# Block 2's attention emitted as a pipeline over heads, with TensorE held to the order of emission

## The chip, the cores and the metric

One core of one Trainium2 chip runs the whole program in one launch. The metric is device time in microseconds (us). The kernel is written in Python for a tile framework: the program traces instructions for five engines (TensorE for matrix multiplies and transposes, VectorE for elementwise work and reductions, ScalarE for activation functions and copies, GpSimd, SyncE for DMA issues), a scheduler puts the instructions of each engine into one fixed order, and on the chip every engine works through its own order and waits on semaphores where an operand or a buffer is not ready.

## The reference, cut to what matters

The program computes two transformer blocks in float32 on 512 tokens of width 1024. The change is in the second block, in two of its three attention branches:

```python
h = rms_norm(x, g_norm);  proj = h @ w_in          # q_a k_a v_a ... z_a c_q c_kv ... gate_logits
# branch a: 8 heads of 64, causal and restricted to the top 256 keys of an index score
q_a = partial_rope(rms_norm(q_a, g_qn_a)); k_a = partial_rope(rms_norm(k_a, g_kn_a))
o_a = dsa_attention(q_a, k_a, v_a, q_i, k_i, w_i)  # softmax(q k^T + mask) v, in blocks of 128 queries
# branch b: 8 heads of 96 (64 + 32 rotary), values of 64, causal
q_b = rms_norm(rms_norm(c_q) @ w_uq, g_qn_b); k_b = rms_norm([k_nope, k_rope], g_kn_b)   # then rotary
o_b = causal_attention(q_b, k_b, v_b)
# branch m: cross attention on a memory of 256 tokens
ys = [o_a * silu(z_a), o_b * silu(z_b), o_m * silu(z_m)]
merged = sum over n of sigmoid(gate_logits_n) * (ys_n @ w_branch_n)
x = x + merged @ w_out
```

## The kernel before

**Dense work.** A float32 product of the dense layers is made of three matmuls in the fast float32 form: both operands are split into a high and a low part, and high-high, high-low and low-high are added up in PSUM (`dense`, `dense_tok`). A weight slice is loaded into `wraw`, ScalarE writes its high part `whi`, VectorE the low part `wlo` (`unit`, with high priority). One step of a dense stream is 24 matmuls as a rule: eight slices of 128 rows by three.

**Attention.** Scores of one head for a block b of 128 queries go against the 128(b+1) keys up to that block, b = 0 to 3. `attend` makes one unit, a pair of heads e = 0, 1 for one block. For each head: the scores into a PSUM bank; VectorE adds the mask, writes the result `at_sm` and takes the row maximum `at_mx` in one instruction (L1567); ScalarE takes the exponential with the sum `at_su`; VectorE takes the reciprocal (L1552) and multiplies (`normalise`); TensorE turns the 128x128 pieces into a second bank (`tr`, L191); and that is copied to `at_pt`, by VectorE for e = 0 and by ScalarE for e = 1. After the second head the unit's value products follow (`mm`, L188, tile `y`): 2(b+1) float32 products of 64 columns, each of which stands as two instructions in the trace. When the four blocks of a pair j are done, `branch_in` multiplies the sums by the gate and splits the product into high and low part. PSUM has eight banks; block 2 uses tags mm (2 banks) and q (2) in turn for dense sums (`pm`), y (1) for the attention's output, and p, p, s (3 in all) in turn for scores and transposes (`pt`).

**Streams.** Generators yield after each step, and `weave` draws from several of them: it takes next the one whose count of yields, divided by its number of units, is smallest (`units`, `woven`); a stream that yields None waits, and another is drawn from. The last weave of block 2 (L2048) has three streams: `last_cols` (dense; DU = 53), `attns` (AU = 92, traced with a priority offset AP of 2000 instructions) and `topk` (98; 48 pairs of VectorE's max and match-replace on the index scores, which make the mask of branch a). `attns` does, in order, branch b's heads 0 to 3 (`latent_attn(0)`), then norms, rotary and transposes of the queries and keys of heads 4 to 7 (`latent_prep(1)`), their attention, the norms, rotary and transposes of branch a's queries and keys (`sparse_prep`), and branch a's attention (`sparse_attn`: 4 pairs by 4 blocks). `last_cols` makes the projections that those need (`latent_cols(1)`, `run`), the gates `za`, and the gated sums of branches m and b (`branch`) and the gates of branch a (`gates_a`). `need` lets a stream wait until a name stands in the table T.

**What sets TensorE's order.** In this weave `self.pinned` is empty: dense matmuls are chained to one another in the order in which they are traced (`mmd`), and transposes, scores and value products are placed among them by the scheduler, which goes by priority and by its own forecast of when each is ready. Earlier parts of the kernel set `self.pinned` to "p" (`pin`, L198): then every TensorE instruction is tied behind the one traced before it.

**Places.** `head_norm` L1519, `attend` L1555, `branch_in` L1588, `topk` L1757, `latent_prep` L1872, `latent_attn` L1887, `sparse_prep` L1902, `sparse_attn` L1937, `last_cols` L2027, `attns` L2038, the weave L2048.

Of the kernel before, what the change touches and what calls it, by code (L numbers as in the profile page):

```python
# [18 lines left out]
NB = S // 128  # L19
# [6 lines left out]
PRI, AP = 2000, 2000  # L26
# [8 lines left out]
DU, AU = 53, 92  # L35
# [64 lines left out]
class Build:  # L100
# [1418 lines left out]
    def head_norm(self, pool, x, heads, dim, g, nb=4):  # L1519

        ss = self.tile(pool, [128, 32], "hn_ss", 2)[:, 0:nb * heads]
        n = heads * dim
        for b in range(nb):
            sq = self.tile(self.late or pool, [128, 512], "t2", T2)
            self.act(sq[:, :n], x[:, b], AF.Square)
            self.nc.vector.tensor_reduce(ss[:, heads * b:heads * b + heads],
                                         sq[:, :n].rearrange("p (h d) -> p h d", h=heads), AX.X, OP.add)
        self.ts(ss, ss, 1.0 / dim, 1e-6)
        r = self.rsqrt(pool, ss, nb * heads)
        for b in range(nb):  # L1530
            xv = x[:, b].rearrange("p (h d) -> p h d", h=heads)
            self.mul(xv, xv, r[:, heads * b:heads * b + heads, None].to_broadcast([128, heads, dim]))
            self.mul(xv, xv, g[:, None, :].to_broadcast([128, heads, dim]))

# [20 lines left out]
    def attend(self, pool, b, score, v, mask, O):  # L1555
# [3 lines left out]
        n = 128 * (b + 1)  # L1559
        mx = self.tile(pool, [128, 2], "at_mx", 2)  # L1560
        sums = self.tile(pool, [128, 2], "at_su", 2)
        pts = []
        for e in range(2):
# [3 lines left out]
            nc.vector.tensor_tensor_reduce(sm[:, 0:n], p[:, 0:n], mask[:, 0:n], -1.0, 3e38,  # L1567
# [3 lines left out]
            self.normalise(sm[:, 0:n], sums[:, e:e + 1])  # L1571
            p = self.pt()
# [7 lines left out]
            pts.append(PT)  # L1580
            if e:
                for s in range(b + 1):
                    for c in range(2):
                        self.mm(O[64 * c:64 * c + 64, 128 * b:128 * b + 128], v(c, s),
                                pts[c][:, 128 * s:128 * s + 128], s == 0, s == b)
            yield e
# [9 lines left out]
    def block2(self, main, late, xT, kept, out):  # L1596
# [3 lines left out]
        with tc.tile_pool(name="by", bufs=1, reuse_waits=RW) as py, tc.tile_pool(name="b2", bufs=1, reuse_waits=RW) as p2, xd as dram:  # L1600
# [271 lines left out]
            def latent_prep(hf):  # L1872
                for n, name, tag in (("qb", "lq", "s2"), ("kb", "lk", "s3")):
                    yield from need((name, hf))
                    src = T[name, hf]
                    self.head_norm(p2, src, 4, 96, gains[n])
                    self.rope(p2, src.rearrange("p b (h d) -> p b h d", h=4)[:, :, :, 64:96], 4, 8, 16)
                    dst = T[n] = slot(tag, [96, 4, S])
                    yield 0
# [7 lines left out]
            def latent_attn(hf):  # L1887
# [4 lines left out]
                for j in range(2):  # L1892
                    O = self.pt("y")
                    for b in range(NB):
                        n = 128 * (b + 1)
                        yield from self.attend(
                            p2, b, lambda e, p: self.mm(p[:, 0:n], qT[:, 2 * j + e, 128 * b:128 * b + 128], kT[:, 2 * j + e, 0:n]),
                            lambda e, s: vt[:, s, 2 * j + e], cm[:, 384 - 128 * b:512], O)
                    self.branch_in(O, *(t[:, 2 * hf + j] for t in (T["zb"], *T["b"])))


            def sparse_prep(e, n):  # L1902
                yield from need("t" + n)
                t = T["t" + n]
                self.head_norm(p2, t, 8, 64, gains[n])
                self.rope(p2, t.rearrange("p b (h d) -> p b h d", h=8)[:, :, :, 0:16], 8, 0, 8)
                yield 0
                if e == 0:
# [28 lines left out]
            def sparse_attn():  # L1937
# [9 lines left out]
                for j in range(4):  # L1947
                    O = self.pt("y")
                    for b in range(NB):
                        mask = cm[:, 384:512] if b == 0 else madd[:, moff[b]:moff[b] + 128 * (b + 1)]  # L1950
                        yield from self.attend(p2, b, lambda e, p: score(j, b, e, p),
                                               lambda e, s: va[:, s, 128 * j + 64 * e:128 * j + 64 * e + 64], mask, O)

                    self.branch_in(O, *(t[:, j] for t in (T["za"], *T["a"])))
                    T["ya", j] = True
# [58 lines left out]

            tk = topk()
# [97 lines left out]
```

## Time and profile before

| | |
|---|---|
| time, median of 3 runs | 1573.21 us (1572.8 to 1574.99) |
| the profiled execution's own time | 1564.84 us |
| its span, first to last instruction | 1563.1 us |
| TensorE's mean granted clock | 0.995 |
| TensorE matmul busy | 1523.2 us (97%), 8487 instructions |
| TensorE weight load busy | 1234.9 us (79%) |
| VectorE busy | 1087.7 us (70%), 2536 instructions |
| ScalarE busy | 749.3 us (48%) |
| chain that ended last | PE 82%, DVE 10%, ACT 3%, DMA 2%, issue 2% |

How to read it: PE is TensorE's matmul, PEld its weight load, DVE is VectorE, ACT ScalarE, POOL GpSimd. A matmul's end is modelled and matmuls are pipelined, so the record of one overlaps the next: a PE that is busy for a whole window may still be late. What a matmul costs is the distance from its start to the next one's start. The last weave of block 2 runs from about 1136 us to 1500 us of the span; its attention is between 1141 and 1470 us.

### The profile page before, as it was taken

Reading aid. Unit: us, or ns where it says so; the run is one execution under the profiler, and the core shown is the slowest. Engines: PE = TensorE matmul, PEld = TensorE weight load, DVE = VectorE, ACT = ScalarE, POOL = GpSimd, SP = SyncE. Lnnn points to the kernel's source line nnn. Section 1 sums busy time; section 2 is a strip of 40 time slices with the busy share of each in tenths; the row PEclk is TensorE's granted clock in tenths of the full one; section 3 lists DMA queues with packets and bytes.
Section 4 is the critical chain, followed back from the end, with each engine's and each line's share of the span. In section 5 each row is a group of like instructions: output and inputs, shape, how many; then the busy total and the mean of one; then the engine's idle time right before and its main releaser. Section 6 shows DMA issues by size and latency. Waiting matters only on the chain.

```text
span 1563.1 us, 23743 instructions
## 1 busy us (share of the span) xinstructions
PE 1523.2 (97%) x8487; PEld 1234.9 (79%) x8487; DVE 1087.7 (70%) x2536; ACT 749.3 (48%) x1469; POOL 101.0 (6%) x241
## 2 busy tenths in 40 slices
PE   6999999999999999999999999999999999999999
PEld 5777787788788888888888888888877778777787
DVE  7776697889757565534544578879998758765563
ACT  5645555456455444433432444456554445543431
POOL 7000402121000000000000001000000000000000
PEclk9999999999999999999999999999999999999999
DMA  7533122135534133333333334242322213224232
GB/s 249 142 72 81 48 64 53 39 92 147 170 93 131 41 94 92 97 96 100 95 97 99 92 105 106 65 117 77 90 62 66 70 52 85 77 65 128 62 96 100
DMA packets 209591, 144.85 MB, mean 93 GB/s; under 512 B 13492, under 2 KB 190787, under 8 KB 208960
## 3 DMA queue, kind: packets, MB, share of 16 engines
q1 hardware_dynamic: 208000, 141.66, 32.1%
q0 software_dynamic: 1280, 1.52, 0.4%
q8 instruction: 67, 1.10, 0.3%
q14 instruction: 52, 0.43, 0.1%
q10 hardware_dynamic: 192, 0.14, 0.0%
HBM read 134.90 MB, written 8.39 MB: 92 GB/s over the span
## 4 chain that ended last, share of the span: by engine, by line
PE 82%; DVE 10%; ACT 3%; DMA 2%; issue 2%; SPq 0%; DVEq 0%; ACTq 0%
PE mm L180 38%; PE q L180 27%; PE p L188 4%; PE p L191 3%; PE y L188 3%; DVE wlo L158 2%; PE s L188 2%; PE s L180 2%; PE q L188 2%; PE s L191 1%; PE q L191 1%; DVE St L158 1%; DVE lqk L158 1%; ACT whi L155 1%; DMA kvraw<-k_kept 1%
## 5 line engine op out<-in xcount | busy, mean ns | idle before, releaser
L155 ACT ACTIVATE whi<-wraw 128x512 fp32r<-128x512 f32 (+2 forms) x472 | 292.2, 621 | 499.6 <-PE mm L180 206.2
L158 DVE TENSOR_TENSOR wlo<-wraw,whi 128x512 fp32r<-128x512 f32 (+2 forms) x472 | 320.5, 680 | 187.9 <-ACT whi L155 180.3
L180 PE MATMUL mm<-hh,whi 128*128 128x512 f32 (+1 forms) x744 | 275.8, 387 | 1.3 <-DVE hh L158 1.3
L180 PE MATMUL mm<-hh,wlo 128*128 128x512 f32 (+1 forms) x680 | 261.6, 385 | 0.0
L180 PE MATMUL mm<-hl,whi 128*128 128x512 f32 x616 | 243.9, 396 | 0.0
L180 PEld LDWEIGHTS mm<-hh,whi 128*128 128x128 f32 x744 | 136.7, 190 | 27.4 <-issue 2.8
L180 PEld LDWEIGHTS mm<-hh,wlo 128*128 128x128 f32 x680 | 128.6, 189 | 24.1 <-issue 1.0
L180 PEld LDWEIGHTS mm<-hl,whi 128*128 128x128 f32 x616 | 116.2, 189 | 23.1 <-issue 2.6
L180 PE MATMUL q<-hh,whi 128*128 128x512 f32 x288 | 112.9, 392 | 0.0
L180 PE MATMUL q<-hl,whi 128*128 128x512 f32 x288 | 112.4, 390 | 0.0
L180 PE MATMUL q<-hh,wlo 128*128 128x512 f32 x288 | 112.4, 390 | 0.0
L180 PE MATMUL q<-whi,hh 128*128 128x512 f32 (+2 forms) x176 | 65.6, 385 | 0.0
L180 PE MATMUL mm<-whi,hh 128*128 128x512 f32 (+2 forms) x168 | 64.2, 389 | 0.0
L180 PEld LDWEIGHTS q<-hh,whi 128*128 128x128 f32 x288 | 54.1, 188 | 11.6 <-issue 0.7
L180 PEld LDWEIGHTS q<-hl,whi 128*128 128x128 f32 x288 | 54.1, 188 | 11.1 <-issue 0.2
L180 PEld LDWEIGHTS q<-hh,wlo 128*128 128x128 f32 x288 | 54.1, 188 | 11.1
L180 PE MATMUL q<-wlo,hh 128*128 128x512 f32 (+2 forms) x160 | 61.0, 381 | 0.0
L180 PE MATMUL mm<-wlo,hh 128*128 128x512 f32 (+2 forms) x152 | 58.4, 384 | 0.0
L180 PE MATMUL q<-whi,hl 128*128 128x512 f32 (+2 forms) x144 | 55.0, 382 | 0.0
L155 ACT ACTIVATE at_sm<-at_sm,at_mx 128x128 f32<-128x128 f32 (+3 forms) x64 | 35.7, 558 | 34.9 <-DVE at_mx L1567 34.3
L180 PE MATMUL mm<-whi,hl 128*128 128x512 f32 (+2 forms) x136 | 52.1, 383 | 0.0
L176 DVE SCALAR_TENSOR_TENSOR fy<-fc,vcols,fy 128x512 f32<-128x512 f32 x44 | 33.0, 752 | 8.9 <-ACT fy L155 8.1
(710 smaller groups left out, 3139.6 us busy)
## 6 DMA issues: line engine op xcount, KB each, us to landing
wraw<-in_w_in_dram SPq DMA_DIRECT2D x172, 256.0 KB, 2.9
wraw<-in_f_up_dram SPq DMA_DIRECT2D x88, 256.0 KB, 2.9
wraw<-in_f_down_dram SPq DMA_DIRECT2D x40, 256.0 KB, 2.8
wraw<-in_x_wkv_dram SPq DMA_DIRECT2D x32, 256.0 KB, 3.1
wraw<-in_w_out_dram SPq DMA_DIRECT2D x32, 256.0 KB, 2.8
wraw<-in_w_branch_dram SPq DMA_DIRECT2D x24, 256.0 KB, 2.7
wraw<-in_w_mem_kv_dram SPq DMA_DIRECT2D x16, 256.0 KB, 4.8
wraw<-in_x_wq_dram SPq DMA_DIRECT2D x16, 256.0 KB, 2.8
```

The source lines that it names most:

```text
L155: self.pin("a", self.nc.scalar.activation(out, in_, func, **kw))
L158: self.pin("v", self.nc.vector.tensor_tensor(out, a, b, op=op))
L176: self.pin("v", self.nc.vector.scalar_tensor_tensor(out, a, s, b, op0=op0, op1=op1))
L180: ins = self.nc.tensor.matmul(out, lhsT=a, rhs=b, start=start, stop=stop)
L188: self.pin("p", self.nc.tensor.matmul(out, lhsT=a, rhs=b, start=start, stop=stop))
L191: self.pin("p", self.nc.tensor.transpose(out, in_, self.ident if ident is None else ident))
```

## The change

The same instructions are made, on the same operands; their order of emission and the tie on TensorE change.

- `attend` takes all units of a branch. One step turns the head whose scores were made two steps earlier, makes the scores of a new head, and then emits the value products of a unit of which both heads were turned by the end of the step before. `at_sm` keeps its two buffers and `at_pt` its three.
- `head_norm` becomes a generator in five parts (`head_norms`), `latent_prep` and `sparse_prep` are cut into norms and transposes, and `along` draws one part of the next norms after each step of the attention.
- In `last_cols` the projection `tqa` comes before `branch("m")`, six steps of that branch come before `prep1` is waited for and six after `tka`, and two of the eight gates of branch a come after `begin("a", 0, range(3))`. `attns` waits for "ym read" before it reuses that slot.
- `self.pinned` is "p" during the last weave. DU goes from 53 to 50; the weave before it has 20 units for its attention stream in place of 16.

```diff
-DU, AU = 53, 92
+DU, AU = 50, 92
...
+    def head_norms(self, pool, x, heads, dim, g, nb=4):
...
+            if b % 2:
+                yield 0
         self.ts(ss, ss, 1.0 / dim, 1e-6)
         r = self.rsqrt(pool, ss, nb * heads)
+        yield 0
...
-    def attend(self, pool, b, score, v, mask, O):
+    def attend(self, pool, units):
...
+        heads, ready = [], []
+        O = {}
+
+        def scores(u, e, mx, sums):
...
+        def turned(u, e, sm):
...
+        def values(u, pts):
+            j, b, _, v, _, o, done = u
+            if b == 0:
+                O[j] = o()
+            for s in range(b + 1):
+                for c in range(2):
+                    self.mm(O[j][64 * c:64 * c + 64, 128 * b:128 * b + 128], v(c, s),
+                            pts[c][:, 128 * s:128 * s + 128], s == 0, s == b)
+            if b == NB - 1:
+                done(O.pop(j))
+
+        def step(new):
+            pair = ready.pop(0) if len(ready) and len(ready[0][1]) == 2 else None
+            if len(heads) == 2 or not new:
+                u, e, sm = heads.pop(0)
+                PT = turned(u, e, sm)
+                if e == 0:
+                    ready.append((u, [PT]))
+                else:
+                    ready[-1][1].append(PT)
+            if new:
+                u, e, mx, sums = new
+                heads.append((u, e, scores(u, e, mx, sums)))
+            if pair:
+                values(*pair)
+
+        for u in units:
+            mx = self.tile(pool, [128, 2], "at_mx", 2)
+            sums = self.tile(pool, [128, 2], "at_su", 2)
+            for e in range(2):
+                step((u, e, mx, sums))
+                yield e
+        while heads:
+            step(None)
+            yield 0
+        while ready:
+            values(*ready.pop(0))
...
+            def along(main, side, n):
+
+                for at in main:
+                    for _ in part(side, n):
+                        pass
+                    yield at
+                for at in side:
+                    if at is None:
+                        yield None
...
-            weave(self.units(7, chain(latent_cols(0), values_a())), self.units(16, latent_prep(0), AP))
+            weave(self.units(7, chain(latent_cols(0), values_a())), self.units(20, along(latent_turn(0), latent_norms(0), 2), AP))
             def last_cols():
-                yield from chain(latent_cols(1), branch("m"), run(0, 512, "tqa", "s1", evac))
+                yield from chain(latent_cols(1), run(0, 512, "tqa", "s1", evac))
+                bm = branch("m")
+                yield from part(bm, 6)
                 yield from need("prep1")
                 yield from run(512, 512, "tka", "lqk", evac)
+                yield from bm
+                T["ym read"] = True
                 yield from need("yb")
                 yield from chain(gate(2120, "za", "s4"), branch("b"))
                 yield from need("prepa")
-                yield from gates_a()
+                ga = gates_a()
+                yield from part(ga, 6)
                 yield from need(("ya", 2))
                 T["early"] = begin("a", 0, range(3))
+                yield from ga
 
             def attns():
-                yield from chain(latent_attn(0), latent_prep(1))
+                yield from along(latent_attn(0), latent_norms(1), 1)
+                yield from latent_turn(1)
                 T["prep1"] = True
-                yield from latent_attn(1)
+                yield from along(latent_attn(1), chain(sparse_norm("qa"), sparse_norm("ka")), 1)
                 T["yb"] = True
+                yield from need("ym read")
                 yield from chain(sparse_prep(0, "qa"), sparse_prep(1, "ka"))
...
+            self.pinned = "p"
             weave(self.units(DU, last_cols()), self.units(AU, attns(), AP), self.units(98, tk))
+            self.pinned = ""
```

## Rows read from the trace of the kernel before

**Rows 1.** Busy time of each engine by stretch: a stretch of the first block that is dense work alone, latent heads 0 to 3, the norms of heads 4 to 7, latent heads 4 to 7, and branch a's attention. Columns: stretch, length, busy us and records of PE, PEld, DVE, ACT, POOL, then granted clock, DMA share and GB/s.

```profile
600.00:920.00 320.00, 320.00 (x1413) 264.96 (x1413) 163.04 (x242) 125.43 (x195) 3.44 (x23) 1.00 0.33 96
1141.00:1205.00 64.00, 64.00 (x331) 46.17 (x331) 56.52 (x155) 32.69 (x81) 3.10 (x8) 1.00 0.23 59
1205.00:1229.00 24.00, 23.99 (x114) 19.52 (x113) 23.61 (x70) 9.73 (x18) 0.00 (x0) 1.00 0.33 88
1229.00:1281.00 52.00, 51.92 (x280) 35.10 (x279) 31.06 (x92) 23.20 (x58) 1.04 (x2) 1.00 0.19 52
1342.00:1474.00 132.00, 131.17 (x695) 98.06 (x696) 86.39 (x221) 61.10 (x137) 0.00 (x0) 1.00 0.30 81
```

**Rows 2.** The same view for matmuls of single lines between 1125 and 1474 us, one answer after another: L180 (dense), L191 (transposes), L188 (scores and value products), and, last, the matmuls that read or write tile XL (36 of the 52 are 384 wide). Columns: stretch, length, PE busy us and records, clock, DMA share, GB/s.

```profile
1125.00:1474.00 349.00, 272.74 (x1069) 1.00 0.28 74
...
1125.00:1474.00 349.00, 42.80 (x256) 1.00 0.28 74
...
1125.00:1474.00 349.00, 73.40 (x448) 1.00 0.28 74
...
1125.00:1474.00 349.00, 13.00 (x52) 1.00 0.28 74
```

**Rows 3.** TensorE's timeline: the first and the last of 24 dense matmuls in a row, and the two instructions of one latent score of 384 keys with the matmul behind them. Columns: start us, length us, engine, line, operation, out<-in, shapes, count.

```profile
1079.62 0.39 PE L180 MATMUL mm<-hh,whi 128*128 128x512 f32 x1
...
1084.83 0.39 PE L180 MATMUL mm<-hh,wlo 128*128 128x512 f32 x1
...
1242.20 0.81 PE L188 MATMUL p<-s,s 96*128 96x384 f32 x2
1242.85 0.27 PE L191 MATMUL p<-ident,at_sm 128*128 128x128 f32 x1
```

**Rows 4.** The chain that ended last, in order of time: eight transposes in a row (start us, us, what).

```profile
988.81 0.87 PE p L191 x8
```

**Rows 5.** TensorE's timeline: bursts of value products and the matmul behind each; the first and the last rows are the first and the last of 54 bursts between 1125 and 1474 us (24 of 2 instructions, 4 of 4, 8 of 6, 3 of 8, 5 of 10, 3 of 12, 7 of 14).

```profile
1145.71 0.44 PE L188 MATMUL y<-at_pt,lv 128*64 128x128 f32 x4
1146.08 0.45 PE L180 MATMUL q<-whi,XL 128*128 128x384 f32 x1
...
1166.71 0.43 PE L188 MATMUL y<-at_pt,lv 128*64 128x128 f32 x2
1167.07 0.50 PE L180 MATMUL mm<-hh,whi 128*128 128x512 f32 x1
1167.50 1.09 PE L188 MATMUL y<-at_pt,lv 128*64 128x128 f32 x14
1168.52 0.50 PE L180 MATMUL mm<-hl,whi 128*128 128x512 f32 x1
...
1468.82 1.09 PE L188 MATMUL y<-at_pt,s 128*64 128x128 f32 x14
```

**Rows 6.** TensorE's timeline: the four matmuls of branch a's preparation before which the engine stood idle; in brackets the idle us and what ended it.

```profile
1306.98 0.30 PE L191 MATMUL p<-ident,s 128*128 128x128 f32 x1 [0.47 <-DVE s L158]
...
1312.73 0.63 PE L191 MATMUL p<-ident,s 128*128 128x128 f32 x4 [0.37 <-DVE ym L158]
...
1334.77 0.95 PE L191 MATMUL p<-ident,lqk 128*128 128x128 f32 x7 [0.75 <-DVE lqk L158]
...
1342.58 0.39 PE L188 MATMUL p<-s,ym 128*128 128x256 f32 x1 [0.59 <-ACT s L155]
```

**Rows 7.** Who waited for whom between 1125 and 1474 us, weight loads of scores (us in total, times, longest).

```profile
PEld s L188 <- ACT at_pt L155: 2.5, 8, 0.6
...
PEld p L188 <- ACT at_pt L155: 2.1, 7, 0.4
...
PEld p L188 <- DVE at_mx L1567: 1.5, 7, 0.3
```

**Rows 8.** Timeline of several engines at the end of branch a's attention: the last head's scores, maximum, exponential, normalisation, transposes and copy; then, after the last value products, the three instructions of `branch_in`.

```profile
1463.67 0.40 PE L188 MATMUL s<-kl,ym 128*128 128x512 f32 x1
...
1464.11 0.69 DVE L1567 CUSTOM_DVE_ANT_0 at_sm<-s,madd 128x512 f32<-128x512 f32 x1 [0.48 <-PE s L188]
...
1464.84 0.72 ACT L155 ACTIVATE at_sm<-at_sm,at_mx 128x512 f32<-128x512 f32 x1 [1.04 <-DVE at_mx L1567]
...
1465.89 0.49 DVE L171 TENSOR_SCALAR at_sm<-at_sm,at_su 128x512 f32<-128x512 f32 x1
...
1467.36 0.60 PE L191 MATMUL p<-ident,at_sm 128*128 128x128 f32 x4
...
1468.14 0.58 ACT L155 ACTIVATE at_pt<-p 128x512 f32<-128x512 f32 x1
...
1469.94 0.69 DVE L158 TENSOR_TENSOR t<-y,s 128x512 f32<-128x512 f32 x1 [0.96 <-PE y L188]
...
1470.67 0.63 ACT L155 ACTIVATE ym<-t 128x512 fp32r<-128x512 f32 x1 [1.94 <-DVE t L158]
...
1471.33 0.69 DVE L158 TENSOR_TENSOR ym<-t,ym 128x512 fp32r<-128x512 f32 x1 [0.70 <-ACT ym L155]
```

**Rows 9.** VectorE: the top-k's busy time while latent heads 0 to 3 run (stretch, length, DVE us and records, POOL); one group of rotary products between 1080 and 1474 us (count, busy us, mean ns); and two of them in the timeline (start us, us).

```profile
1141.00:1205.00 64.00, 24.42 (x53) 0.00 (x0) 1.00 0.23 59
...
L158 DVE TENSOR_TENSOR rope<-lqk,sin 128x256 f32<-128x256 f32 x10 | 3.9, 415 | 0.0
...
1135.26 0.75 DVE L158 TENSOR_TENSOR rope<-lqk,sin 128x256 f32<-128x256 f32 x2
```

More of the change, by code (lines that the diff above doesn't have):

```diff
@@ L1519, in head_norm @@
     def head_norm(self, pool, x, heads, dim, g, nb=4):
+        for _ in self.head_norms(pool, x, heads, dim, g, nb):
+            pass
+    def head_norms(self, pool, x, heads, dim, g, nb=4):
         ss = self.tile(pool, [128, 32], "hn_ss", 2)[:, 0:nb * heads]
@@ L1553, in normalise @@
         self.ts(P, P, s)
-    def attend(self, pool, b, score, v, mask, O):
+    def attend(self, pool, units):
         nc = self.nc
[L1559 to L1563, printed above, removed]
+        heads, ready = [], []
+        O = {}
+        def scores(u, e, mx, sums):
+            j, b, score, v, mask = u[:5]
+            n = 128 * (b + 1)
             p = self.pt()
@@ L1571, in attend @@
             self.normalise(sm[:, 0:n], sums[:, e:e + 1])
+            return sm
+        def turned(u, e, sm):
+            b = u[1]
+            n = 128 * (b + 1)
             p = self.pt()
@@ L1579, in attend @@
                 nc.vector.tensor_copy(PT[:, 0:n], p[:, 0:n])
[L1580 to L1586, printed above, removed]
+            return PT
+        def values(u, pts):
[30 more added lines that the diff above has]
+            step(None)
+            yield 0
+        while ready:
+            values(*ready.pop(0))
     def branch_in(self, O, z, hi, lo):
@@ L1891, in latent_attn, with done, unit, sparse_norm @@
                     T["b"] = (Y[:, 0], Y[:, 1])
[L1892 to L1902, printed above, removed]
+                def done(j):
+                    return lambda O: self.branch_in(O, *(t[:, 2 * hf + j] for t in (T["zb"], *T["b"])))
+                def unit(j, b):
+                    n = 128 * (b + 1)
+                    return (j, b, lambda e, p: self.mm(p[:, 0:n], qT[:, 2 * j + e, 128 * b:128 * b + 128], kT[:, 2 * j + e, 0:n]),
+                            lambda e, s: vt[:, s, 2 * j + e], lambda: cm[:, 384 - 128 * b:512], lambda: self.pt("y"), done(j))
+                yield from self.attend(p2, [unit(j, b) for j in range(2) for b in range(NB)])
+            def sparse_norm(n):
                 yield from need("t" + n)
                 t = T["t" + n]
-                self.head_norm(p2, t, 8, 64, gains[n])
+                yield from self.head_norms(p2, t, 8, 64, gains[n])
                 self.rope(p2, t.rearrange("p b (h d) -> p b h d", h=8)[:, :, :, 0:16], 8, 0, 8)
+                T["normed", n] = True
                 yield 0
+            def sparse_prep(e, n):
+                yield from need(("normed", n))
+                t = T["t" + n]
                 if e == 0:
@@ L1945, in score, with done, put, unit @@
                     self.mm(p[:, 0:n], q[:, 2 * j + e, bs], kl[j][:, e, 0:n], False, True)
[L1947 to L1955, printed above, removed]
+                def done(j):
+                    def put(O):
+                        self.branch_in(O, *(t[:, j] for t in (T["za"], *T["a"])))
+                        T["ya", j] = True
+                    return put
+                def unit(j, b):
+                    return (j, b, lambda e, p: score(j, b, e, p), lambda e, s: va[:, s, 128 * j + 64 * e:128 * j + 64 * e + 64],
+                            lambda: cm[:, 384:512] if b == 0 else madd[:, moff[b]:moff[b] + 128 * (b + 1)],
+                            lambda: self.pt("y"), done(j))
+                yield from self.attend(p2, [unit(j, b) for j in range(4) for b in range(NB)])
             def gate_block(n, m, tg):
```

17 lines of the change are left out of this document (12 added, 5 removed).

## The prediction

> **What bounds the kernel now.** I read the page first: PE is busy 97% and makes 82% of the chain that ended last, so a step pays only if it shortens TensorE's own stream. Busy time does not show how much there is to win, because records overlap; so next came the busy times by stretch, then counts by line, and then the distances from one matmul's start to the next in the timeline. In the first block's dense stretch PE is busy without a break, and in the last weave it is too [rows 1]; yet the weight loads fill 0.83 of the one and 0.72 and 0.74 of the two attention stretches (46.17 of 64, 98.06 of 132).
>
> The work between 1125 and 1474 us at its own pace: dense, 23 distances in 5.21 us, 0.2265 us each [rows 3]; of 1069 dense matmuls 36 are 384 wide [rows 2], so 1033 x 0.2265 + 36 x 0.17 = 240.1. Transposes, 0.109 each [rows 4], 256 of them: 27.9. Latent scores, 0.65 for 384 keys [rows 3], 0.217 for each 128, 32 heads and blocks of 2.5 on average: 17.4. Branch a's scores, two fast matmuls 256, 256, 384 or 512 wide, at the dense pace: 8 x 2 x 0.62 = 10.0. Value products: 12 instructions more cost 1.02 - 0.36 us [rows 5], 0.055 each, and 320 of them (448 less 128 scores [rows 2]): 17.6. Sum 313.0 of 349 us, so **36 us are lost**, and that is the most that any order could win. Behind 1474 us dense work runs on, and nothing there is touched but the very end.
>
> Where the 36 us go. A burst of two value products takes 0.36 us where two at pace take 0.11: each burst starts with 0.25 (0.15 for a burst of four, 0.37 - 0.22), and its first start comes later behind the matmul in front (0.43 for 0.23 [rows 5]; I count 0.1, half of it, as that row may hold a wait). There are 54 bursts for 32 units, since the first product of a unit needs only the first head's copy and the scheduler puts it early: 54 x 0.35 = 18.9 us. Four waits stand before branch a's preparation, 2.2 us [rows 6]. The other 14.9 us I spread over the entries from dense work into transposes or scores, 104 by count in the timeline: 0.143 each, small waits included.
>
> **The change part by part.** The sum is made against the profiled execution, 1564.84 us (span 1563.1); the median shown is 8.4 higher, and the difference is added to the median.
>
> *Order on TensorE.* Walking the three streams' yields (47 dense steps of 1/50, 86 attention steps of 1/92) gives 45 groups of attention work with dense steps of 24 matmuls, 5.4 us, between them; 27 groups hold two scores. Within a group the order is transposes, scores, values. All value products of a unit stand together, after both copies: 32 bursts of 4, 8, 12 or 16, 32 x (0.15 + 0.1) = 8.0, so 10.9 saved; were the start 0.25 for these too, 7.7. Entries from dense work: 45 x 0.143 = 6.4, so 8.5 saved; if half of that loss goes with heads and not with entries, 4. No arithmetic is added or taken away.
>
> *Norms beside the attention.* The waits of 2.2 us go: `sparse_prep` finds its rows normalised. VectorE's and ScalarE's work stays the same and moves forward; the cover is the dense step between a head's scores and its transposes. Unhindered, one 512-key head takes from its last score at 1464.0 to 1466.4, 2.4 us [rows 8], two one after the other less than 5.4.
>
> *What is late next.* The tie makes every instruction behind a waiting one wait, dense work included. (1) The score of the second step in a group takes the bank that the first step's transposes used (three banks, two per step), so it waits for that copy. The trace has such waits: 22 of them, 6.1 us, 0.28 on average, 0.6 at most [rows 7]. The 27 groups with two scores, at 0.2 since value products often stand between: 5.4 us; bounds 0 and 27 x 0.6 = 16.2. (2) Where the pipeline runs empty. The last head of a branch has nothing between its transposes and its values: four transposes from 1467.36, the copy done at 1468.72, values at 1468.82 [rows 8, 5], 1.0 us beyond the transposes' own 0.44. That comes three times. At the end of latent heads 4 to 7 the last score, too, stands in the same group as its transposes: 2.4 less 0.44 and 0.81 of other work, 1.2. At the weave's end branch a's last product waits for `branch_in`, with all dense work tied behind it: the sum read at 1469.94, high part at 1471.30, low part at 1472.02 [rows 8], where before gates of branch a still filled that time; about 2.0. Together 3.0 + 1.2 + 2.0 = 6.2 (bounds 4 and 9).
>
> *Moved loads.* `tqa`'s weights are issued on SP ahead of branch m's in place of behind; DMA share is 0.23 to 0.33 there [rows 1], and the next weights are asked for a step ahead, so I cost it at nothing; a late slice would hold one dense step. `kl`'s clearing on GpSimd is covered (3.1 us of 64 busy [rows 1]). The weave before, with 20 units and norms in parts, starts no score before the same dense steps: nothing, 1 us either way.
>
> Sum after: 8.0 + 6.4 + 5.4 + 6.2 = 26.0 us lost for 36.0: **10.0 us saved, 1563 us**.
>
> **The rivals.** *The pipeline never waits.* No bank waits, entries at 0.09: 8.0 + 4.0 + 6.2 = 18.2 lost, 17.8 saved, 1555. For it: a full dense step between scores and transposes. Against: three banks are few.
>
> *Bank waits at their longest.* Each of 27 groups loses 0.6: 8.0 + 6.4 + 16.2 + 6.2 = 36.8, no gain, 1574. For it: VectorE runs in order, and the copy stands behind whatever it is doing, at 88% busy in 1141 to 1205 us [rows 1]. Against: the average in rows 7 is half of that. [...]
>
> *VectorE becomes the bound, slower.* Place: latent heads 0 to 3. VectorE worked 56.5 us there and 23.6 in the norms behind it, 80.1 in all [rows 1]. Now both fall into one stretch, which takes TensorE 12 x 0.17 + 8 x 5.44 of dense work, 8.7 of scores, 4.4 of transposes, 6.4 of values and 1.4 of entries: 66.4 us. It is 13.7 us short unless the top-k, 24.4 us of that stretch [rows 9], is put behind it. Tied matmuls wait for the shortfall: if the top-k gives way by less than 3.7 us, the 10.0 are gone; not at all, 3.7 us slower, 1577. For it: the top-k held that share beside the attention although the latter has priority. Against: it is needed only 29 dense steps into the weave, and VectorE has 20 us free between 1229 and 1281 [rows 1].
>
> VectorE's records overlap: two rotary products of 0.415 take 0.75 [rows 9]. [...]
>
> *Nothing is gained.* The losses are not of the order but of each instruction's kind, and come back in the new order: 1573. Against: the bursts of rows 5 show that a split costs.
>
> **How the numbers follow.** Forecast 0.50, never waits 0.12, longest bank waits 0.13, VectorE the bound 0.18, nothing gained 0.07. What this kernel's times can tell from no change is some 0.2%, 3.1 us. Faster: 0.50 + 0.12 + 0.02 of the bank rival = 0.64. Same: the bank rival's 0.09, nothing gained 0.07, 0.02 of VectorE's = 0.18. Slower: 0.16 + 0.02 = 0.18. The forecast's own range, from the bounds: 7.7 + 4 + 2.2 - 9 (tails) - 3 at worst and 10.9 + 10.9 + 2.2 - 4 - 2 at best, 2 to 18 saved, most of it 1557 to 1569. With the rivals, 8 in 10: 1556 to 1577.
>
> **What would show it.** Value products in the weave in 32 bursts or a few more, none of two instructions; four waits of rows 6 gone; waits of scores on the copies `at_pt` near 5 us and none over 1; idle TensorE of 1 to 2 us three times, at the ends of the three attentions, the longest before branch a's last product; the top-k's last instructions later than before, among latent heads 4 to 7. Wrong, if the weave's TensorE idles before transposes on `at_sm` in many groups (VectorE the bound), if VectorE is over 95% busy through latent heads 0 to 3 while TensorE waits, or if the bursts of values stay at 54.

## The result, and the profile after

The changed kernel takes 1560.43 us (median of 9 runs, 1554.19 to 1565.83), the kernel before 1572.8 (9 runs, 1566.05 to 1576.74). The medians lie 12.4 us apart. The ratio of the runs is 0.9933, 95% interval [0.9913, 0.9953]: 10.5 us faster, where 10.0 were forecast.

The page of the changed kernel (busy time, and the chain that ended last, by engine):

```profile
PE 1515.9 (97%) x8487; PEld 1242.7 (80%) x8487; DVE 1086.4 (70%) x2536; ACT 748.3 (48%) x1469; POOL 99.5 (6%) x241
...
PE 85%; DVE 9%; ACT 3%; issue 2%; DMA 1%; DVEq 0%; ACTq 0%; SPq 0%
```

TensorE is as full as before, and the two profiled executions hardly differ: 1563.55 us against 1564.84. TensorE's order is the same in both kernels up to the first matmul on `XL` (`latent_cols(0)`), so I cut each trace there and at the program's last matmul. Busy time by stretch, first of the kernel before, then of the changed one (columns as in [rows 1]):

```profile
0.00:440.00 440.00, 409.52 (x3111) 335.65 (x3112) 345.88 (x887) 246.36 (x491) 84.98 (x166) 0.98 0.37 105
...
1100.14:1558.99 458.85, 455.99 (x2264) 351.72 (x2263) 327.31 (x815) 208.09 (x434) 4.14 (x10) 1.00 0.29 79
```

```profile
0.00:440.00 440.00, 407.70 (x3064) 334.14 (x3065) 342.13 (x878) 240.62 (x483) 83.43 (x166) 0.96 0.37 103
...
1109.62:1557.66 448.04, 441.31 (x2265) 353.56 (x2263) 324.17 (x815) 207.21 (x434) 4.29 (x10) 1.00 0.29 81
...
1152.60:1220.00 67.40, 67.00 (x358) 51.45 (x356) 66.51 (x204) 35.78 (x86) 2.21 (x6) 1.00 0.25 67
```

In the first 440 us, which the change does not touch, the granted clock is 0.98 in the one and 0.96 in the other, and 47 fewer matmul records stand in it; the cut comes 9.5 us later. From the cut to the end it is 458.85 against 448.04: 10.8 us saved. All runs below are read by this stretch too. At the paces of the prediction its work (1488 dense matmuls 512 wide, 72 of 384, and the transposes, scores and value products) takes 422.1 us, so 36.7 us were lost before and 25.9 after; idle time is only a part of that. In this stretch the granted clock is 1.00 in both.

TensorE's waits in the changed kernel from 1109 to 1510 us (us in total, times, longest):

```profile
PE q L180 <- ACT ym L155: 1.4, 1, 1.4
PE p L191 <- DVE at_sm L171: 1.2, 1, 1.2
PE y L188 <- ACT at_pt L155: 1.0, 3, 0.3
PE p L188 <- ACT at_pt L155: 0.7, 2, 0.4
PE s L188 <- DVE at_pt L1596: 0.5, 1, 0.5
PE s L191 <- DVE lv L158: 0.4, 1, 0.4
```

The four waits of [rows 6] are gone; a new one, 0.4 us on `lv`, stands in branch a's preparation, and what is new besides are the ends, the first three rows. Weight loads of scores, same stretch, where [rows 7] stood:

```profile
PEld p L188 <- ACT at_pt L155: 1.5, 4, 0.6
PEld p L188 <- DVE at_pt L1596: 0.9, 4, 0.3
PEld s L188 <- ACT at_pt L155: 0.8, 2, 0.4
...
PEld s L188 <- DVE at_pt L1596: 0.8, 1, 0.8
```

Eleven waits, 4.0 us, none over 0.8. These are rows of the weight load, which runs beside the matmuls (busy 80% and 97% of the span). TensorE itself is idle before scores for a copy four times, 1.4 us in all (two rows above and one of 0.2). TensorE's and the other engines' timeline: a burst of value products with the matmul behind it ([rows 5]), and the ends of the attentions of latent heads 0 to 3, 4 to 7 and of branch a ([rows 8]):

```profile
1217.86 0.68 DVE L1813 MATCH_REPLACE8 madd<-m,madd 128x512 f32<-128x512 f32 x1
...
1218.38 0.43 PE L188 MATMUL y<-at_pt,lv 128*64 128x128 f32 x2
1219.14 1.09 PE L188 MATMUL y<-at_pt,lv 128*64 128x128 f32 x14 [0.32 <-ACT at_pt L155]
1220.16 0.64 PE L191 MATMUL p<-ident,lqk 128*96 128x128 f32 x4
...
1315.39 0.63 PE L191 MATMUL p<-ident,at_sm 128*128 128x128 f32 x4 [1.22 <-DVE at_sm L171]
1315.95 0.43 PE L188 MATMUL y<-at_pt,lv 128*64 128x128 f32 x2
1316.70 1.09 PE L188 MATMUL y<-at_pt,lv 128*64 128x128 f32 x14 [0.32 <-ACT at_pt L155]
...
1427.82 1.09 PE L188 MATMUL y<-at_pt,s 128*64 128x128 f32 x16
1428.85 0.33 PE L191 MATMUL p<-ident,at_sm 128*128 128x128 f32 x1
...
1493.00 1.09 PE L188 MATMUL y<-at_pt,s 128*64 128x128 f32 x14 [0.32 <-ACT at_pt L155]
...
1495.54 0.50 PE L180 MATMUL q<-ym,whi 128*128 128x512 f32 x1 [1.44 <-ACT ym L155]
```

Bursts are whole now, of 4, 8, 12 and 16 instructions, eight of each by count (where a burst stands as 2 and 14, its second part waited for the second head's copy). At the last row nothing covers the chain of `branch_in`: TensorE is idle for 1.44 us.

### The profile page after: what moved, and what is told of

It reads as the page before. It is cut to its first block, busy times and chain, and to the rows that moved or that the text cites. A ratio compares the mean times of both kernels' runs of the same rounds, so it can differ in the third digit from the quotient of the medians.

```text
span 1561.8 us, 23725 instructions
## 1 busy us (share of the span) xinstructions
PE 1515.9 (97%) x8487; PEld 1242.7 (80%) x8487; DVE 1086.4 (70%) x2536; ACT 748.3 (48%) x1469; POOL 99.5 (6%) x241
## 4 chain that ended last, share of the span: by engine, by line
PE 85%; DVE 9%; ACT 3%; issue 2%; DMA 1%; DVEq 0%; ACTq 0%; SPq 0%
PE mm L180 40%; PE q L180 27%; PE p L188 4%; PE p L191 3%; PE y L188 3%; PE s L180 2%; PE s L188 2%; DVE wlo L158 2%; PE q L188 2%; PE q L191 1%; PE s L191 1%; ACT whi L155 1%; DVE St L158 1%; DVE lqk L158 1%; DVE madd L1813 1%
## 5 line engine op out<-in xcount | busy, mean ns | idle before, releaser
L180 PE MATMUL mm<-hh,whi 128*128 128x512 f32 (+1 forms) x760 | 284.9, 391 | 1.3 <-DVE hh L158 1.3
L180 PE MATMUL mm<-hh,wlo 128*128 128x512 f32 (+1 forms) x696 | 267.2, 384 | 0.0
L180 PE MATMUL mm<-hl,whi 128*128 128x512 f32 x632 | 248.4, 393 | 0.0
L180 PEld LDWEIGHTS mm<-hh,whi 128*128 128x128 f32 x760 | 140.9, 192 | 29.3 <-issue 3.4
L180 PEld LDWEIGHTS mm<-hh,wlo 128*128 128x128 f32 x696 | 132.6, 190 | 25.7
L180 PEld LDWEIGHTS mm<-hl,whi 128*128 128x128 f32 x632 | 120.0, 190 | 22.2 <-issue 0.5
L180 PE MATMUL q<-hh,whi 128*128 128x512 f32 x272 | 106.2, 391 | 0.0
L180 PE MATMUL q<-hh,wlo 128*128 128x512 f32 x272 | 106.0, 390 | 0.0
L180 PE MATMUL q<-hl,whi 128*128 128x512 f32 x272 | 106.0, 390 | 0.0
L180 PE MATMUL q<-whi,hh 128*128 128x512 f32 (+2 forms) x176 | 66.4, 389 | 0.0
L180 PE MATMUL mm<-whi,hh 128*128 128x512 f32 (+2 forms) x168 | 65.2, 395 | 0.0
L180 PE MATMUL q<-wlo,hh 128*128 128x512 f32 (+2 forms) x160 | 61.1, 382 | 0.0
L180 PEld LDWEIGHTS q<-hh,wlo 128*128 128x128 f32 x272 | 51.1, 188 | 10.7
L180 PEld LDWEIGHTS q<-hh,whi 128*128 128x128 f32 x272 | 51.1, 188 | 10.5
L180 PEld LDWEIGHTS q<-hl,whi 128*128 128x128 f32 x272 | 51.1, 188 | 10.4
L180 PE MATMUL mm<-wlo,hh 128*128 128x512 f32 (+2 forms) x152 | 57.9, 381 | 0.0
L180 PE MATMUL q<-whi,hl 128*128 128x512 f32 (+2 forms) x144 | 54.7, 380 | 0.0
L180 PE MATMUL mm<-whi,hl 128*128 128x512 f32 (+2 forms) x136 | 51.6, 380 | 0.0
```

Source lines behind the costliest of these rows:

```text
L180: ins = self.nc.tensor.matmul(out, lhsT=a, rhs=b, start=start, stop=stop)
```

## The experiments

Time is the median, and each ratio is taken against runs of the kernel before made beside it; "stretch" runs from the cut to the last matmul. E11 is one execution. The intervals reach some 3 us to either side, so differences of a few us between two of the changed kernels (E1, E5, E6) rest on the stretch alone, which is one profiled execution each.

| run | time us (runs) | ratio to before, 95% | stretch us | to the changed kernel |
|---|---|---|---|---|
| before | 1572.8 (9) | | 458.9 | +10.8 |
| changed | 1560.43 (9) | 0.9933 [0.9913, 0.9953] | 448.0 | |
| E1 no tie | 1562.74 (7) | 0.9946 [0.9924, 0.9968] | 452.4 | +4.3 |
| E2 tie alone | 1831.72 (2) | 1.1658 [1.1617, 1.1699] | 720.6 | +272.6 |
| E3 norms in turn | 1590.27 (6) | 1.0127 [1.0102, 1.0152] | 476.9 | +28.9 |
| E4 first product early | 1574.92 (12) | 1.0023 [1.0008, 1.0038] | 465.4 | +17.3 |
| E5 halves in turn | 1564.01 (9) | 0.9961 [0.9945, 0.9976] | 451.9 | +3.8 |
| E6 46 units | 1557.79 (6) | 0.9913 [0.9893, 0.9934] | 444.2 | -3.8 |
| E7 paired steps | 1554.26 (6) | 0.9890 [0.9869, 0.9912] | 441.8 | -6.2 |
| E8 53 units | 1567.47 (12) | 0.9981 [0.9964, 0.9998] | 455.7 | +7.7 |
| E9 top-k first | 1586.95 (6) | 1.0111 [1.0086, 1.0135] | 476.7 | +28.7 |
| E10 paired, no tie | 1574.56 (12) | 1.0026 [1.0010, 1.0041] | 461.4 | +13.4 |
| E11 two by two | 1555.57 (1) | | 448.3 | +0.2 |

**E1, the order without the tie; E2, the tie without the order.**

```diff
# E1, to the changed kernel
-            self.pinned = "p"
             weave(self.units(DU, last_cols()), self.units(AU, attns(), AP), self.units(98, tk))
-            self.pinned = ""
# E2, to the kernel before
+            self.pinned = "p"
             weave(self.units(DU, last_cols()), self.units(AU, attns(), AP), self.units(98, tk))
+            self.pinned = ""
```

> The changed kernel without the tie on TensorE in the last weave; pipeline, norms and counts stay. Theory (the order of tracing makes the gain, the tie is only its guard): a unit's value products become ready together, since both copies are traced a step ahead, so the scheduler keeps them together, 32 to 40 bursts; the waits of scores on the copies get shorter, dense work fills the ends; 1556 to 1564 us. Rival (the tie makes the gain): the scheduler takes value products and transposes apart again, over 50 bursts and some 100 entries from dense work, 1568 to 1574 us.

> The kernel before with the tie on TensorE in the last weave and nothing else. Theory (the tie needs the pipeline): each head's transposes stand right behind its scores in the order of tracing, and the tied engine waits out mask, exponential and normalisation, 2.4 us for 512 keys and some 1.6 for 128, mean 2.0, 64 times, 128 us; before each unit's values the second copy, some 0.8, 32 times, 26 us; less some 15 us of losses that the tie takes away: about 1710 us (1670 to 1750). Rival (the tie alone makes the gain): 1558 to 1566 us.

E1 keeps 6.5 of the 10.8 us by the stretch, and its time lies within the theory's 1556 to 1564, but not for its reason. In its timeline stand 47 bursts of value products (32 tied), ten of them of one product, and 85 entries from dense work into transposes or scores (48 tied); what it wins back is the ends, where the scheduler puts dense work (at the last one 0.7 us of idle time are left). E2 settles that the tie alone is ruin, and by more than I had said. TensorE's waits in E2, 1125 to 1800 us, and the timeline behind one of them:

```profile
PE p L191 <- DVE at_sm L171: 98.5, 43, 3.4
PE s L191 <- DVE at_sm L171: 48.5, 21, 3.1
```

```profile
1163.05 0.69 PE L191 MATMUL s<-ident,at_sm 128*128 128x128 f32 x2 [2.27 <-DVE at_sm L171]
...
1165.85 0.63 PE L180 MATMUL mm<-wlo,XL 128*128 128x512 f32 x1
1166.27 0.63 PE L180 MATMUL mm<-whi,s 128*128 128x512 f32 x1
```

The busy times of the dense matmuls behind that wait (columns as in [rows 1]):

```profile
1165.25:1167.12 1.87, 1.87 (x5) 1.49 (x5) 1.80 (x4) 0.00 (x0) 0.00 (x0) 0.50 0.00 0
```

All 64 heads wait, 147 us, and two norms 21: 168 of the 262 us that the stretch is longer than before. I had left out what follows: behind an idle of 2.27 us the next dense matmuls stand 0.42 us apart, and 0.23 only from 1167.5 on. In the row of 1165.25 to 1167.12 us the granted clock is 0.50; from 1167.75 to 1170 us it is 1.00, and over E2's whole stretch 0.82. The other 94 us were not taken apart.

**E3, norms a whole tensor at a time between the attentions.**

```diff
-                yield from along(latent_attn(0), latent_norms(1), 1)
-                yield from latent_turn(1)
+                yield from latent_attn(0)
...
+                for n in norm_by_norm(latent_norms(1), 6):
+                    yield n
+                    yield from part(turn, 4)
...
-                yield from along(latent_attn(1), chain(sparse_norm("qa"), sparse_norm("ka")), 1)
+                yield from latent_attn(1)
...
+                    for _ in sparse_norm(n):
+                        pass
+                    yield 0
+                    yield from sparse_prep(e, n)
```

> The changed kernel with the norms traced one whole tensor at a time between the attentions, as before, and tied as after. Theory (beside the attention they are covered, behind it TensorE waits for them): each of four norms is 10 to 12 us of VectorE with one dense step of 5.4 us in front of its transposes; the first two wait some 5 us each, branch a's two 1 to 3 each: 8 to 16 us slower than the changed kernel, 1568 to 1576 us, with idle TensorE before transposes of lqk and s. Rival (the scheduler draws norms ahead into VectorE's gaps wherever they are traced): 1560 to 1563 us, the four waits of the kernel before at the most (2.2 us).

Theory in kind, twice its size. E3's waits, 1100 to 1577 us:

```profile
PE p L191 <- DVE lqk L158: 11.1, 2, 10.9
PE p L191 <- DVE s L158: 7.2, 1, 7.2
PE p L191 <- DVE at_sm L171: 4.8, 4, 1.2
```

A single norm is waited for in full, 10.9 us. With 7.2 for branch a's queries, and three heads more that wait for their own softmax at the ends (4.8 less 1.2 us), that makes 21.7 of the 28.9; the rest I did not take apart (the stretch's granted clock is 0.98). So under the tie the norms beside the attention are no refinement: without them the change would lose.

**E8, the number of units back.**

```diff
-DU, AU = 50, 92
+DU, AU = 53, 92
```

> The changed kernel with the 53 units of the kernel before for its dense stream, nothing else. By the yields the dense stream then runs ahead: at the end of latent heads 4 to 7 three heads are turned in the same group as their own scores (one in the changed kernel), at the end of branch a four (none in the changed kernel), with no dense step between. Theory (each such head costs its softmax chain, 2.4 us for 512 keys less 0.8 of other work): 2 + 4 = 6 heads x 1.6 = 9.6 us more than the changed kernel, 1570 us (1567 to 1572), so the gain of the change hangs on this number. Rival (the number of units only shifts where the same waits fall): within 2 us, 1558 to 1563.

Theory, a little under its size: 7.7 of the gain of 10.8 us hang on this number. At 53 the dense stream is used up before branch a's last heads. TensorE waits for `at_sm` four times, 5.3 us, where the changed kernel does once, 1.2 us: three heads more, not six, and 4.1 of the 7.7 us; the rest was not taken apart. E8's timeline there, one of two such rows:

```profile
1488.22 0.55 PE L191 MATMUL p<-ident,at_sm 128*128 128x128 f32 x3 [1.47 <-DVE at_sm L171]
```

**E9, the top-k put ahead of the attention.**

```diff
-            weave(self.units(DU, last_cols()), self.units(AU, attns(), AP), self.units(98, tk))
+            weave(self.units(DU, last_cols()), self.units(AU, attns(), AP), self.units(98, tk, AP + 400))
```

> The changed kernel with the top-k stream traced at a priority 400 above the attention's: in VectorE's order all 48 pairs then stand ahead of the first mask of latent heads 0 to 3. Theory (VectorE is full from 1080 us to the end of latent heads 0 to 3, 39.65 and 39.97 of 40 us before, 66.5 of 67.4 in them, and TensorE is covered only because the top-k fills what the attention leaves): the 22 us of top-k that stood in latent heads 0 to 3 push the norms and turns of heads 0 to 3 back, TensorE has no other work tied free in front of them, and 10 to 22 us are lost: 1570 to 1582 us, with idle TensorE before transposes of lqk. Rival (VectorE's order does not matter, as the sum of its work is 70% of the span): 1558 to 1564 us.

Worse than the theory's worst, at an earlier place than it named. E9, busy time of one stretch and the longest waits from 1080 to 1180 us:

```profile
1100.00:1140.00 40.00, 24.96 (x92) 19.06 (x91) 36.90 (x107) 15.02 (x33) 0.00 (x0) 0.74 0.12 33
```

```profile
PE p L191 <- DVE ckv L171: 10.6, 4, 10.1
PE p L191 <- DVE lqk L158: 3.6, 1, 3.6
```

TensorE idles for the latents' norm already, then for heads 0 to 3, and the granted clock falls to 0.74 with it. In latent heads 0 to 3 VectorE then has room that nothing needs (31.56 of 40 us busy from 1180 to 1220). Where the top-k gives way, TensorE is idle for 0.4 us in that stretch of the changed kernel; where it does not, 28.7 us are lost.

**E4, E5 and E11: what a burst of value products costs.**

```diff
# E4: one product a step ahead
+            self.mm(O[j][0:64, 128 * b:128 * b + 128], v(0, 0), pts[0][:, 0:128], True, b == 0)
...
+            half = ready[0] if len(ready) and len(ready[0][1]) == 1 else None
...
+            if half:
+                first(*half)
# E5: the first head's blocks, then the second's
-            for s in range(b + 1):
-                for c in range(2):
+            for c in range(2):
+                for s in range(b + 1):
# E11: two blocks of the first head, two of the second, and so on
+            for s, c in [(s, c) for s0 in (0, 2) for c in range(2) for s in (s0, s0 + 1) if s <= b]:
```

> The changed kernel with the first value product of each unit one step ahead of the others: 64 bursts in place of 32, no other work. Theory (a burst costs 0.25 us, 0.15 at its start and 0.1 behind the matmul ahead of it): 32 x 0.25 = 8 us more than the changed kernel, 1568 us; at 0.35, as before's bursts of two cost, 11 more, 1571. Rival (it is not the burst that costs, but the waits that stood there): within 2 us of the changed kernel, 1558 to 1563.

> The changed kernel with a unit's value products in another order: all blocks of the first head (rows 0 to 63 of the output bank), then all of the second (rows 64 to 127), in place of the two heads by turns. Same instructions, same bursts. In the traces so far a burst of 2 instructions (one product) takes as long as one of 4 (0.36 and 0.37 us), one of 6 as long as one of 8 (0.58 and 0.59). Theory (products of the two heads run side by side, because they fill different halves of TensorE's columns, and one alone costs what two cost): by turns 0.109 us a product, in turn 0.218: 160 x 0.109 = 17 us more than the changed kernel, some 1577 us. Rival (0.055 us an instruction in any order, and what a burst costs is its start alone): within 2 us of it, 1558 to 1563.

> The changed kernel with a unit's value products by twos: two blocks of the first head, two of the second, then the other blocks in the same way. In the run with the halves in turn, bursts of 8 instructions, two products to each half in a row, cost nothing more (0.59 us), those of 12 and 16, three and four in a row, 0.27 and 0.49 more. Theory (two products in a row to one half are absorbed, the third and the fourth wait 0.12 us each): bursts of 12 at 0.81 and of 16 at 1.03 us, as by turns. Rival (each change of the halves that does not come after every product costs, and the burst of 8 only hides it at its end): bursts of 12 and 16 near 0.9 and 1.25 us, half of the way to the halves in turn.

E4 is well above both of its numbers. Its timeline has 61 bursts, 37 of them of one product; a burst of 14 and one of 2, each with the matmul behind it:

```profile
1431.86 1.09 PE L188 MATMUL y<-at_pt,s 128*64 128x128 f32 x14
1432.88 0.33 PE L191 MATMUL p<-ident,at_sm 128*128 128x128 f32 x1
...
1434.67 0.40 PE L188 MATMUL y<-at_pt,s 128*64 128x128 f32 x2 [1.22 <-DVE at_su L1561]
1435.00 0.50 PE L180 MATMUL mm<-hh,whi 128*128 128x512 f32 x1
1435.34 0.40 PE L180 MATMUL mm<-hl,whi 128*128 128x512 f32 x1
```

The burst of 14 takes 1.02 us, as one of 16 does in the changed kernel (1.03): the product taken out saves nothing there and costs 0.36 and 0.1 elsewhere. 29 more bursts at 0.46 are 13.3, two waits of 1.22 such as this one 2.4. That leaves 1.6 of the 17.3. The last two rows hold a price that I had not seen: behind the first dense matmul after a burst the next one starts 0.34 us later, where the pace is 0.2265. In E4 33 bursts stand in front of dense work, in the changed kernel 17: 16 x 0.11 = 1.8. E5 and E11 ask why one product costs what two cost. E5's bursts of 16 and 8, then E11's of 16, each with the matmul behind it:

```profile
1426.78 1.58 PE L188 MATMUL y<-at_pt,s 128*64 128x128 f32 x16
1428.29 0.33 PE L191 MATMUL p<-ident,at_sm 128*128 128x128 f32 x1
...
1442.25 0.66 PE L188 MATMUL y<-at_pt,s 128*64 128x128 f32 x8
1442.84 0.55 PE L191 MATMUL s<-ident,at_sm 128*128 128x128 f32 x3
```

```profile
1419.80 1.14 PE L188 MATMUL y<-at_pt,s 128*64 128x128 f32 x16
1420.88 0.33 PE L191 MATMUL p<-ident,at_sm 128*128 128x128 f32 x1
```

By turns a burst of 16 takes 1.03 us, in turn 1.51, by twos 1.08; one of 8 takes 0.59 in turn as well as by turns. E5's theory, 17 us, and its rival, 2, both missed (3.8): the order matters, but two products in a row to one half are all but absorbed. E11 bears that out, to 0.05 us.

**E6, E7 and E10: can the ends be filled?**

```diff
# E6
-DU, AU = 50, 92
+DU, AU = 46, 92
# E7
-DU, AU = 50, 92
+DU, AU = 48, 46
...
                 step((u, e, mx, sums))
-                yield e
+            yield 0
         while heads:
             step(None)
-            yield 0
+        yield 0
...
-                    yield 0
+                    if j % 2:
+                        yield 0
...
-                yield from along(latent_attn(0), latent_norms(1), 1)
+                yield from along(latent_attn(0), latent_norms(1), 2)
```

> The changed kernel with 46 units for the dense stream in place of 50, nothing else. By the streams' yields a dense step then stands between the last turns and the last values of all three attentions, two dense steps follow the last values, and one group at the start of branch a holds scores and their own turns. Theory (the ends where the pipeline runs empty cost 0.75, 2.0 and 2.3 us in the trace of the changed kernel, and dense work can fill them): 5.0 saved, up to 2.4 lost at branch a's start: 3 to 5 us faster than the changed kernel, 1556 to 1558 us. Rival (the ends are waits on a chain that ends the weave anyway, and dense work held back for them is late behind them): 1560 to 1564 us.

> The changed kernel with both heads of a unit in one step of the stream, so that every group holds turn, scores, values of the unit before, turn, scores; units 48 and 46. By the yields no group holds a turn with its own scores or values with their own turns, 44 groups, three dense steps behind the last values. Theory (the second scores of a group wait for the copy of the first turn, because the values stand behind them in half of the groups; with the values between, the copy is done): the waits of scores on at_pt, 4.0 us in the weight loads' rows of the changed kernel, shrink to 1, and the ends, 5.0 us, are filled: 7 us faster than the changed kernel, 1551 to 1556 us. Rival (VectorE cannot finish two heads' masks and normalisations in one dense step of 5.4 us in latent heads 0 to 3, where it is the fullest engine, and turns wait): TensorE idle before transposes on at_sm in many groups of 1140 to 1220 us, 1561 to 1570 us.

> The kernel with paired steps without the tie on TensorE in the last weave. Theory (the order of tracing makes the gain; the tie keeps the value products together, 47 bursts without it and 32 with it in the changed kernel, 0.46 us for each split, but costs waits that dense work could fill): 15 x 0.46 = 7 less 2 to 3 of waits filled: 4 us slower than with the tie, 1557 to 1560 us. Rival (with no run-empty ends left the tie has nothing to cost and nothing to give): 1552 to 1556 us.

In E7 `latent_turn(1)` yields after every second turn too, and the second `along` draws two parts as well. E10 is E7 without the tie, as E1 is the changed kernel without it.

E6 does what its theory says. Of the three ends 0.7 us are left, before branch a's last product and now for `t`; a new wait stands at branch a's preparation, where 16 transposes in one group wait for a bank (E6, 1100 to 1510 us):

```profile
PE p L191 <- DVE ym L158: 2.8, 1, 2.8
PE q L180 <- DVE t L176: 0.7, 1, 0.7
```

E7 is the best of all, and its interval lies wholly below the changed kernel's, if barely (0.9912 against 0.9913). Its longest wait in the same stretch, and the weight loads of scores:

```profile
PE s L191 <- DVE at_sm L171: 1.0, 1, 1.0
```

```profile
PEld p L188 <- DVE at_pt L1596: 1.4, 7, 0.2
PEld s L188 <- DVE at_pt L1596: 1.1, 3, 0.8
```

The ends are filled, but for the same 0.7 us; the scores' waits shrink from 4.0 to 2.5 us, not to 1. VectorE did not become the bound: the one wait on `at_sm` is at the second group of all, behind a short dense step. E10 refutes what E1 had seemed to say, and misses both numbers set for it. Without the tie the scheduler takes the paired steps apart into 57 bursts, 29 of one product, and 86 entries from dense work (44 with the tie). 25 more bursts at 0.46 are 11.5; 27 more of them in front of dense work at 0.11 are 3.0; the 42 more entries, with the way back into dense work, 2.6; and one wait for `at_sm` 2.1: together 19.2 of the 19.6 us that E10's stretch is longer than E7's.

## Why the prediction was right

Time, sign and range hold: 1563 forecast, 1560.43 measured, and 25.9 us lost where 26.0 were summed up. The groups of attention work are 48, for 45 walked, and 27 of them hold two scores, as walked. That the sum agrees so closely is in part luck: one term was sized from rows of the weight load, another is a remainder, and their errors cancel. The terms, one by one:

- *Bursts.* Forecast 32 bursts, 8.0 us. Found 32, at 0.15 beyond the pace of their products and 0.09 in front: 7.7. In the trace of before, summed over its 54, 17.9. Right, though the price of a split was put together wrongly: 0.25 + 0.1, where a lone product costs 0.46, as E4 shows; the 22 splits fewer at 0.46 are 10.1, the difference of the two sums 10.2.
- *Entries.* Forecast 45 x 0.143 = 6.4. Found 48; what the other terms leave of the 25.9 us is 9.2, 0.19 each. Both prices are remainders, and the entry is the wrong place for them: from dense work into transposes or scores, rows with idle time aside, the distances are 0.03 us over the pace on average before and 0.01 after. Much of it is the dense matmul behind a burst, 0.11 us (E4): 50 bursts stood in front of dense work before and 17 after, which is 3.6 us of the saving. The 0.43 us of [rows 5] hold this 0.11 and the 0.09 in front of the next burst, not a wait.
- *Bank waits.* Forecast 27 x 0.2 = 5.4. Found 11, 4.0 us, 0.36 each: fewer and longer, since values stand between in 12 of the 27 groups. But these rows, like [rows 7] from which the price was taken, are of weight loads. TensorE itself is idle before scores for 1.4 us, and in the trace of before, where [rows 7] add up to 6.1 us (1.5 of them for the maximum, not for a copy), for a copy once, 0.2 us. So the term was too high by 1.4 to 4.0 us.
- *Ends.* Forecast 6.2. Found 0.75, 2.0 and 2.3 (the burst's time beyond its pace, with the idle before it): 5.0, each at its place. E6 and E7 show that all but 0.7 could be had.
- *Norms.* The four waits are gone; E3 shows the cover to be worth more than the 2.2 us that I credited, since under the tie the alternative is not [rows 6] but 18 us (10.9 + 7.2).
- *Moved loads.* Costed at nothing, and none of TensorE's waits from 1109 to 1510 us ends on a DMA.
- *Profile and median.* I added the 8.4 us by which the profiled execution of before lay under its median. The two traces differ by as much (9.5 us) in the untouched first part, so I read it as a matter of that part; the saving does come on the median.

One statement failed: that the top-k ends among latent heads 4 to 7. Its last instruction stands at 1217.86, 65 us behind the first latent score (52 before) but still in latent heads 0 to 3. The step that failed is the sum of 80.1 us for VectorE: the 23.6 us of the norms' stretch were not all norms. VectorE's groups there, in the kernel before, 1205 to 1229 us (busy us, mean ns, idle before):

```profile
L158 DVE TENSOR_TENSOR wlo<-wraw,whi 128x512 fp32r<-128x512 f32 x8 | 5.5, 687 | 0.0
...
L176 DVE SCALAR_TENSOR_TENSOR XL<-tg,q 128x512 f32<-128x512 f32 x3 | 2.0, 682 | 0.0
...
L158 DVE TENSOR_TENSOR tg<-mm,rb 128x512 f32<-128x512 f32 x2 | 1.4, 680 | 0.0
```

These 8.9 us belong to dense work; without them the shortfall is 4.8 us, not 13.7. The top-k gave way by 1.9 us only, 24.4 us in that stretch before [rows 9] and 22.5 after: less than the 3.7 at which I had written the gain off, and the gain is there. In the row of 1152.60 to 1220.00 us of the changed kernel VectorE is busy 66.51 of 67.4 us with TensorE idle 0.4. So the rival of VectorE as the bound was closer than 0.18 reads: the stretch is full to the brim, and E9 shows that 22 us of top-k in the wrong place cost 28.7.

The rivals: never waits (1555) fell to the ends, and E7, which takes most of them away, comes out at 1554; bank waits at their longest fell to the eleven waits; that nothing is gained fell to the interval.

## What to carry to other kernels

In these runs a tie to the order of emission paid where the emission itself puts independent work between a producer and its consumer: the same two lines made the kernel before 260 us slower, and were worth 4.3 us in the changed kernel and 20 us with paired steps; with norms in turn the whole change would have lost 18. Then look where the pipeline runs empty, and let the streams' rates leave a dense step there (50 units for 53 was 7.7 us; from there 46 units gave 3.8, and paired steps with 48 gave 6.2). And compare two profiles by the stretch that changed, between two matmuls that both have: here the whole spans differed by 1.3 us, and the stretch by 10.8.

## What the runs showed of the hardware

Float32 value products of 64 columns, by turns into rows 0 to 63 and 64 to 127 of a bank: a burst takes 0.37, 0.59, 0.81 and 1.03 us for 4, 8, 12 and 16 instructions, 0.15 + 0.22 for each pair of products, and an odd last product costs as much as a pair (0.36 for one in [rows 5], 1.02 for seven in E4). I read the single records as the products of the two heads running side by side: by turns the instructions start in pairs, 0.007 us apart and 0.109 behind the pair ahead (changed kernel, from 1203.57 us), while those of a lone product start 0.16 apart (before, 1166.71 us). The rows show 64 columns for each product (128*64, beside 128*128 for the dense ones); the record does not name which, so the different halves of E5's theory stay a reading. Two products in a row to one half cost nothing more in E5's bursts of 8 and 0.05 us in E11's of 16, the third and fourth in E5 some 0.12 each. Of the 0.15 us 0.05 stand between the first two pairs and 0.1 behind the last. Then comes 0.11 in the next dense matmul, or 0.055 in the next transpose (0.164 us for 0.109 in the changed kernel). What makes the times in front of a burst and behind it no run took apart, and why a second product in a row is absorbed stays open.

In E2 and E9 idle time was paid for twice: TensorE's granted clock is 0.82 over E2's stretch and 0.74 in E9's row of 1100 to 1140 us, in both of which it waited for VectorE, and dense matmuls stood 0.42 us apart behind 2.27 us of idle time in E2 (0.2265 is the pace), those 384 wide 0.32 behind 2.16 us in E9 (384/512 of the pace is 0.17). The ends of the changed kernel, 1.44 us of idle time at the longest, left the clock at 1.00 (1485 to 1497 us). I had priced waits by their idle time alone.
